# Weight splits on two engines instead of three, and layer-1 scores in fp32 row tiles

## Chip, core and metric

The kernel runs on one core of a Trainium2 chip. The metric is the device time of one launch in microseconds, from before the first instruction to after the last; the host's work on the layout of the weights is not in it. The kernel before takes 675.95 us (median of 3 runs, 675.43 to 677.0).

## The reference

The program is a decoder of two layers on one sequence of 256 tokens with 1024 features, in fp32. Layer 0 is stick-breaking attention with 16 heads of 64, layer 1 is native sparse attention (NSA) with 16 query heads over 4 key groups. Both have an MLP with a squared ReLU and 4096 hidden features. Keys and values of layer 1 come from the stream after layer 0. They feed three branches: 15 compressed blocks of 32 tokens (through a GELU MLP with `cmp_w1`), selected blocks, and a sliding window. With 256 tokens the top-16 choice takes all four blocks and the window of 512 takes all tokens, so the selected and the window branch are both plain causal softmax over their own keys.

```python
def stick_breaking_attention(h, w_qkv, w_o):
    ...
        z = jnp.einsum('bqhd,bshd->bhqs', q_blk, k).astype(jnp.float32) * scale
        causal = key_pos[None, :] < t[:, None]
        log_1m = jnp.where(causal, jax.nn.log_sigmoid(-z), 0.0)
        excl = lax.cumsum(log_1m, axis=3, reverse=True) - log_1m
        a = jnp.where(causal, jnp.exp(jax.nn.log_sigmoid(z) + excl), 0.0)
    ...
def nsa_attention(h, w_q, gate_b, w_o, shared):
    ...
        return jnp.stack([o_cmp, o_sel, o_win], axis=2).reshape(b, Q_BLOCK, 3, NSA_HEADS, DH)
    ...
    out = jnp.einsum('bsch,bschd->bshd', gates.astype(o.dtype), o).reshape(b, s, NSA_HEADS * DH)
    return out @ w_o
    ...
    for layer in range(DEPTH):
        hn = rms_norm(h, norm_gain[layer, 0])
        if layer < N_A_LAYERS:
            h = h + stick_breaking_attention(hn, sb_w_qkv[layer], sb_w_o[layer])
        else:
            j = layer - N_A_LAYERS
            h = h + nsa_attention(hn, nsa_w_q[j], nsa_gate_b[j], nsa_w_o[j], shared)
        h = h + sqrelu_mlp(rms_norm(h, norm_gain[layer, 1]), mlp_w1[layer], mlp_w2[layer])
        if layer == N_A_LAYERS - 1:
            shared = nsa_shared_kv(h, kv_norm, nsa_w_kv, cmp_pos, cmp_w1, cmp_w2)
```

## The kernel before

**Products and weights.** Large products are made of fp32r matmuls. A weight or an activation is split into a high part in fp32r and a low part, the rest; a product is then three matmuls, high by high, high by low and low by high (`mm3`, matmuls at L312). Weights are streamed by SP in tiles of 1 MB (128 x 2048 in fp32) into three buffers `raw`, in the order in which `feed` was called. Each tile is converted in two halves of 1024 columns: ACT casts the high part `wh` (L256), then DVE or POOL subtracts for the low part `wl` (L263). There are three pairs of wh and wl. The next transfer into a raw buffer is issued once the low part of the tile in it is done (`fetch`, called from `split`), and a tile's conversion waits until the tile three before it has been used by PE (`gone`).

**What sets the order.** PE's order is the order of the code. The order on DVE, ACT and POOL is worked out while the program is built: the class `Order` keeps a clock of its own, a queue of ready steps with ranks, and a cost in ns for each step on each engine that may take it, and it hands a step to the first engine that is free. `put` enters a step, `run` hands steps out, `tick` moves the clock by a matmul's cost and `need` waits for a chain of steps. The chosen order is then fixed in the program. The table `ways` says who may do a conversion: the low part goes to DVE or POOL, and to DVE alone inside the MLPs:

```python
        k = {"D": (150 + 1.045 * m, lo("D")), "G": (185 + 1.67 * m, lo("G"))}
        yield {e: k[e] for e in ways["lo"]}
```

**Stages.** Startup loads x and projects the values of layer 0. Layer 0 goes through the heads in groups of four: `proj` makes queries and keys of a head pair (48 fp32r matmuls `qk`, rotary step L617 into `qkT`), `scores` makes `z` in fp32, as two tiles of 64 rows side by side, `soft` is the stick-breaking softmax (ACT exp and log L633, DVE's evacuation L628, scan L634 and subtraction L635 on 128 x 774, ACT exp L637), `turn` transposes the result (`pa`, L324, copied to `sbt` at L674), and `values` makes `po` in two tiles of 64 columns, which L401 takes to `oT`.

An MLP runs over 8 blocks of 512 hidden features: `first(c)` makes two banks `pu` in 32 matmuls of 512 and 256 columns, `square` makes the squared ReLU and its high part hh (ACT L479) and low part hl (DVE L480), and `second(c)` adds 24 matmuls of 512 to the four banks `acc`. `second(c)` stands one block behind `first`: the code runs first(0), first(1), second(0), first(2), second(1), and so on, and the weights are fed in that order. Blocks 0 and 1 start with the half of the features of x that is transposed (`pt`) and normalised (`xn`, L383) first.

Layer 1 begins with three projections of 512 columns for the keys and values (`kv_proj`, `pk`); keys of the compressed branch are kept twice side by side. `gather_tr` and the following steps build the compressed blocks with their positions and split them into high and low parts; `cw_proj` multiplies them with cmp_w1 (`ph`, 64 matmuls, its weights split as all others), and `gelu` (`hx`, `hu` L1111) and `cmp_turn`, `cmp_kv` give the compressed keys and values. `q_proj` makes the queries of one key group in 48 matmuls (`qp`) and leaves them scaled (`qu`, L968), rotated (stream shuffle L974 and three steps on POOL, `qm`) and split in `qs` (L984). The heads go in eight pairs `p`, and the two heads of a pair share one key group. For a pair:

- `scores` makes `z` in 8 fp32r matmuls, with high and low parts stacked on the 128 rows;
- DVE adds the causal mask, writes `pe` and takes the maximum, in one instruction for each of 8 parts (L1020, `nm`);
- ACT takes 8 exps in SBUF (L1025), DVE inverts the sums (L1039) and multiplies them with the gates (L1041), and POOL (L1047) or DVE (L1048) scales `pe`;
- `turn` transposes `pe` in twelve blocks, four to a PSUM bank (`ptp`), in two steps of two banks and one bank, and ACT or DVE copies each bank to `pT` (L1073);
- `values` makes `po` from pT for two pairs, and `out_part` multiplies with the output weights (`acc`).

Between these steps stand other projections in the code, so that PE has work while a pair's softmax runs. Then come the second MLP and the final norm.

## Time and profile before

| what | value |
|---|---|
| median of 3 runs | 675.95 us (675.43 to 677.0) |
| the profiled execution | 676.55 us |
| its span, first to last instruction | 674.5 us |
| mean granted TensorE clock | 0.968 of full speed |
| PE busy | 625.9 us, 3506 matmuls |
| DVE busy | 450.4 us, 669 instructions |
| ACT busy | 343.4 us, 570 instructions |
| POOL busy | 166.7 us, 116 instructions |
| read from HBM | 106.60 MB, 160 GB/s over the span |

The span is shorter than the execution by 2.05 us, which lie ahead of the first and behind the last instruction. Names such as `wl` are the program's tiles, L263 is line 263 of the code, and `wl<-raw,wh` says that an instruction wrote wl from raw and wh. In a list of waits, `PE pa L324 <- ACT sbe L637: 5.1, 3, 3.1` says that PE, ahead of its transposes into pa, was idle for 5.1 us in 3 waits, 3.1 the longest, and that ACT's writing of sbe released it. In a chain, a row has the start, the length in us and the work. In a group, the number behind x is how many instructions there were, then come their busy time in us and the mean of one in ns; behind the second bar stand the idle time of the engine just before them and what ended it. In a table of stretches, the columns after the stretch are PE, its weight loads, DVE, ACT and POOL, each with busy us and the number of instructions, then the mean granted clock of TensorE, the busy share of the DMA engines and GB/s.

### The profile page before, as it was taken

To read this page: it belongs to the slowest core of one execution; us is meant where nothing else is said; L and a number is where in the kernel's file an instruction comes from. 1 tells how busy PE (TensorE), PEld (TensorE's weight loads), DVE (VectorE), ACT (ScalarE), POOL (GpSimd) and SP (SyncE) were. 2 spreads that over 40 slices of the span, in tenths; PEclk is the share of its full clock that TensorE was granted. 3 is DMA by queue.
4 is the path that set the end of the run, shared out by engine and by line. 5 is a ranking of instruction groups with operands and counts; after the bars stand their busy time and mean duration, and the time that the engine had idled before them with its cause. 6 is when DMAs were issued, how large, how long until landed. Compare 5 with 4: busy or idle time off the path is not lost.

```text
span 674.5 us, 8981 instructions
## 1 busy us (share of the span) xinstructions
PE 625.9 (93%) x3506; PEld 530.4 (79%) x3506; DVE 450.4 (67%) x669; ACT 343.4 (51%) x570; POOL 166.7 (25%) x116
## 2 busy tenths in 40 slices
PE   9998999989999999999996687699989999999995
PEld 6797978768888888888895676477768888888884
DVE  6378886556666656567898897675655666565654
ACT  4754564444554444446555655565444554445442
POOL 2654683100000000004689486324100000000000
PEclk9999999889999999999998878799989999999999
DMA  8963324335555555556445411102443545464501
GB/s 282 359 251 109 128 90 172 127 125 188 187 189 188 189 185 195 185 199 223 151 165 200 172 64 62 64 1 71 153 170 139 194 180 202 181 211 182 209 16 63
DMA packets 17322, 108.22 MB, mean 160 GB/s; under 512 B 2304, under 2 KB 3072, under 8 KB 4992
## 3 DMA queue, kind: packets, MB, share of 16 engines
q1 hardware_dynamic: 16848, 107.11, 44.4%
q8 instruction: 27, 0.44, 0.2%
q10 hardware_dynamic: 432, 0.55, 0.2%
q14 instruction: 15, 0.12, 0.1%
HBM read 106.60 MB, written 1.05 MB: 160 GB/s over the span
## 4 chain that ended last, share of the span: by engine, by line
PE 71%; DVE 14%; ACT 5%; POOL 5%; issue 3%; DMA 2%; SPq 0%; POOLq 0%; ACTq 0%; DVEq 0%
PE acc L312 31%; PE pu L312 26%; DVE wl L263 4%; ACT wh L256 2%; PE po L312 2%; PE qk L312 2%; PE qp L312 2%; PE pk L312 2%; DVE sbs L634 2%; DMA raw<-in_wv 2%; PE ptp L324 2%; PE pv L312 2%; DVE sbe L635 1%; PE z L312 1%; POOL wl L263 1%
## 5 line engine op out<-in xcount | busy, mean ns | idle before, releaser
L263 DVE TENSOR_TENSOR wl<-raw,wh 128x1024 fp32r<-128x1024 f32 (+1 forms) x159 | 208.0, 1324 | 130.1 <-ACT wh L256 127.6
L256 ACT CAST wh<-raw 128x1024 fp32r<-128x1024 f32 (+1 forms) x200 | 200.6, 1030 | 133.4 <-PE acc L312 62.4
L263 POOL TENSOR_TENSOR wl<-raw,wh 128x1024 fp32r<-128x1024 f32 (+1 forms) x41 | 107.1, 2623 | 249.2 <-ACT wh L256 246.6
L312 PE MATMUL pu<-xn,wh 128*128 128x512 f32 x512 | 131.5, 395 | 2.6 <-DVE xn L383 2.2
L312 PEld LDWEIGHTS pu<-xn,wh 128*128 128x128 f32 x512 | 93.9, 189 | 22.5 <-DVE xn L383 5.1
L312 PE MATMUL acc<-wh,hh 128*128 128x512 f32 x256 | 101.5, 396 | 5.1 <-ACT hh L479 5.1
L312 PE MATMUL acc<-wh,hl 128*128 128x512 f32 x256 | 101.2, 395 | 0.8 <-DVE hl L480 0.8
L312 PE MATMUL acc<-wl,hh 128*128 128x512 f32 x256 | 101.2, 395 | 0.0
L312 PEld LDWEIGHTS pu<-xn,wl 128*128 128x128 f32 x512 | 71.7, 192 | 5.8
L312 PE MATMUL pu<-xn,wl 128*128 128x256 f32 x512 | 73.4, 284 | 0.0
L312 PEld LDWEIGHTS acc<-wh,hh 128*128 128x128 f32 x256 | 49.0, 192 | 14.9 <-ACT hh L479 5.5
L312 PEld LDWEIGHTS acc<-wh,hl 128*128 128x128 f32 x256 | 48.8, 191 | 12.2 <-DVE hl L480 1.7
L312 PEld LDWEIGHTS acc<-wl,hh 128*128 128x128 f32 x256 | 48.9, 191 | 9.1
L479 ACT CAST hh<-ms 128x512 fp32r<-128x512 f32 x32 | 19.9, 621 | 62.6 <-DVE ms L478 62.6
L1346 POOL TENSOR_TENSOR r<-v,npow 128x1 f32<-128x1 f32 x2 | 1.5, 771 | 187.5 <-DVE v L1344 187.5
L312 PE MATMUL qk<-xa,wh 128*128 128x256 f32 x256 | 47.3, 286 | 0.0
L312 PE MATMUL acc<-wh,oT 128*128 128x512 f32 x128 | 43.8, 403 | 0.0
L312 PEld LDWEIGHTS qk<-xa,wh 128*128 128x128 f32 x256 | 39.7, 191 | 0.5 <-issue 0.3
L465 ACT COPY mr<-pu 128x256 f32<-128x256 f32 x64 | 23.6, 369 | 25.2 <-PE pu L312 25.2
L312 PE MATMUL qk<-xa,wl 128*128 128x256 f32 x128 | 36.2, 283 | 0.0
L480 DVE TENSOR_TENSOR hl<-ms,hh 128x512 fp32r<-128x512 f32 x32 | 22.1, 692 | 19.3 <-ACT hh L479 19.3
L466 DVE TENSOR_TENSOR mu<-pu,mr 128x256 f32<-128x256 f32 x64 | 26.6, 418 | 7.3 <-ACT mr L465 7.3
(178 smaller groups left out, 884.3 us busy)
## 6 DMA issues: line engine op xcount, KB each, us to landing
raw<-in_w SPq DMA_DIRECT2D x64, 1024.0 KB, 4.8
raw<-in_wqk SPq DMA_DIRECT2D x8, 1024.0 KB, 5.7
raw<-in_wo SPq DMA_DIRECT2D x8, 1024.0 KB, 4.9
raw<-in_wkv SPq DMA_DIRECT2D x6, 1024.0 KB, 4.8
raw<-in_wq SPq DMA_DIRECT2D x4, 1024.0 KB, 4.9
raw<-in_cw SPq DMA_DIRECT2D x4, 1024.0 KB, 4.7
raw<-in_wv SPq DMA_DIRECT2D x2, 1024.0 KB, 6.5
raw<-in_wv SPq DMA_DIRECT2D x3, 512.0 KB, 5.7
```

The costliest lines, as they stand in the source:

```text
L256: nc.scalar.copy(ws.made[j][0][:, r], ws.raws[j][:, r])
L263: (nc.vector if e == "D" else nc.gpsimd).tensor_sub(ws.made[j][1][:, r], ws.raws[j][:, r], f32(ws.made[j][0][:, r]))
L312: nc.tensor.matmul(o_, a, b, start=first, stop=last, skip_group_check=True)
L324: nc.tensor.transpose(o_, a, i)
L465: yield act(256, lambda: nc.scalar.copy(r[:, q], pu[f][:, 256:512]))
L466: yield dve(256, lambda: nc.vector.tensor_add(u[:, q], pu[f][:, 0:256], r[:, q]))
L479: yield act(512, lambda: nc.scalar.copy(hh, sv))
L480: yield dve(512, lambda: nc.vector.tensor_sub(hl, sv, f32(hh)))
L634: yield dve(774, lambda: nc.vector.tensor_tensor_scan(s[:, ::-1], s[:, ::-1], go_on[:, ::-1], 0.0, OP.add, OP.mult), 810)
L635: yield {"D": (956, lambda: nc.vector.tensor_sub(e, e, s)), "G": (1480, lambda: nc.gpsimd.tensor_sub(e, e, s))}
L1346: yield pool(1, lambda: nc.gpsimd.tensor_tensor(r, v, npow, op=OP.pow), 370)
```

## The change

The change has four parts.

1. **Low parts.** The low part of a weight is made on DVE only, in all stages, and so is the subtraction at the end of the stick-breaking softmax. The builder's queue also has two new rules: a step that reads and writes SBUF only on DVE (marked True) is not handed out while such a step of POOL runs, or the other way round (`port`), and steps of low rank can be held back for a time (`calm`).
2. **MLP.** `second` stands two blocks behind `first`: first(0), first(1), first(2), second(0), and so on, with two second products at the end; the weights are fed in that order.
3. **Layer 1, attention.** Queries and keys stay in fp32 and are not split. The two heads of a pair now come from two key groups (the host permutes the columns of the query and gate weights and the rows of the output weights to match), so that the two groups' keys lie one above the other in `kT`, and the scores of the two heads are fp32 matmuls in two tiles of 64 rows, in four PSUM banks. The causal mask is added by four bf16 matmuls (`z<-mask`). DVE takes the maxima from PSUM (L1064, four for a pair), ACT takes the exps from PSUM (L1058). Scaling is done apart for the two halves of the tokens (L1085 on POOL, L1086 on DVE), and `turn` transposes one bank at a time, in three steps, most of them into bank 2. Queries no longer take the scaling step (`qm`, L1016, is made from `qp` with a table that has the norm in it).
4. **Layer 1, projections.** The keys of the two causal branches are projected together, in 512 columns; their values in two projections of 256 columns (`v_proj`) that stand among the turns. The compressed weights are not split: `feed(..., True)` leaves the tile raw, no conversion is made, `cw_proj` takes it in fp32 matmuls of 256 columns in two tiles of 60 columns, and the next transfer into that raw buffer waits for PE. The compressed blocks are not split either.

```diff
+    def may(self, e, x):
+        if x[2][e][2] and self.port["G" if e == "D" else "D"] > self.t:
+            return False
+        return x[0] < 2 or self.calm[e] <= self.t
...
         wa, wb = [], []
         for c in range(NFC):
             wa.append(feed(w1[layer, c], 2048))
-            if c:
-                wb.append(feed(w2[layer, c - 1], 2048))
-        return wa, wb + [feed(w2[layer, NFC - 1], 2048)]
+            if c >= 2:
+                wb.append(feed(w2[layer, c - 2], 2048))
+        return wa, wb + [feed(w2[layer, c], 2048) for c in (NFC - 2, NFC - 1)]
...
+    feed_cw(0)
+    i_q.append(feed(wq[0], 2048))
+    feed_cw(1)
+    feed_cw(2)
+    i_q.append(feed(wq[1], 2048))
+    feed_cw(3)
+    i_vs.append(feed(wvs[0], 2048))
+    i_q.append(feed(wq[2], 2048))
+    i_vs.append(feed(wvs[1], 2048))
+    i_q.append(feed(wq[3], 2048))
...
-    ways = {"hi": "A", "lo": "DG"}
+    ways = {"hi": "A"}
...
-        k = {"D": (150 + 1.045 * m, lo("D")), "G": (185 + 1.67 * m, lo("G"))}
-        yield {e: k[e] for e in ways["lo"]}
+        yield {"D": (150 + 1.045 * m, lo, True)}
...
+        return ws.raws[i] if stream[i][2] else ws.made[i]
 
     def gone(i):
         assert ws.gone == i, (ws.gone, i)
         ws.gone += 1
+        if stream[i][2]:
+            fetch()
...
-        second(*held.pop(0), by_n)
         for c in range(2, NFC):
-            if c in (4, 6):
-                go(inverse_of(c // 2 - 2, r2), 3)
+            if c in (5, 7):
+                go(inverse_of((c - 5) // 2, r2), 3)
             st = begin(c)
             for f in range(2):
                 first(c, st, f, 0, NK)
             gone(wa[c])
             held.append((c, square(st)))
             second(*held.pop(0), by_n)
+        second(*held.pop(0), by_n)
...
-            yield dve(774, lambda: nc.vector.tensor_tensor_scan(s[:, ::-1], s[:, ::-1], go_on[:, ::-1], 0.0, OP.add, OP.mult), 810)
-            yield {"D": (956, lambda: nc.vector.tensor_sub(e, e, s)),
-                   "G": (1480, lambda: nc.gpsimd.tensor_sub(e, e, s))}
+            yield dve(774, lambda: nc.vector.tensor_tensor_scan(s[:, ::-1], s[:, ::-1], go_on[:, ::-1], 0.0, OP.add, OP.mult), 810, True)
+            yield {"D": (956, lambda: nc.vector.tensor_sub(e, e, s), True)}
...
-        def cw_proj(c, i):
+        def cw_proj(n):
+            c, i = divmod(n, 2)
+            o.need(gc_[c])
+            w = W(i_c[c][i])
+            o.tick(90)
             for jj in range(8):
-                w = W(i_c[c][i], jj // 4)
                 j = 8 * i + jj
-                q = ph[:, c * 256:(c + 1) * 256]
-                wh, wl = cut(w, jj * 256, (jj + 1) * 256)
-                mm(q, blk[c][:, j].rearrange("p a m -> p (a m)"), wh, c == 0 and j == 0, False)
-                mm(q[0:DH, :], blk[c][:, j, 0, :], wl, False, j == 15)
+                r = slice(jj % 2 * DH, jj % 2 * DH + M)
+                mm(ph[r, c * 256:(c + 1) * 256], blk[c][:, j, :], w[:, jj * 256:(jj + 1) * 256],
+                   c == 0 and j < 2, j >= 14, 2.0)
+            o.tick(90)
             gone(i_c[c][i])
...
             for hd in range(2):
-                for i in range(2):
-                    mm(z1[hd], x[:, j, hd, P:2 * P], kT[i][:, g, :, :], i == 0, i == 1)
+                r = slice(hd * DH, (hd + 1) * DH)
+                mm(z1[hd], x[r, j, P:2 * P], kT[r, p // 4, :, :], True, False, 2.0)
             for hd in range(2):
-                for i in range(2):
-                    mm(z0[:, hd], x[:, j, hd, 0:P], kT[i][:, g, :, 0:P], hd == 0 and i == 0, i == 1)
...
+            low = mask[:, P:2 * P][:, None, :].to_broadcast([P, 2, P])
+            for z in (z1[0][:, :, P:2 * P], z1[1][:, :, P:2 * P], *z0):
+                mm(z, mask[:, 0:P], low, False, True)
...
+            def ex(hd, t, b):
+                if t:
+                    d, z, i = pe[:, hd, b * 256:(b + 1) * 256], z1[hd][:, b, :], 4 + 2 * hd + b
+                else:
+                    d, z, i = pe[:, hd, 512 + b * P:512 + (b + 1) * P], z0[hd][:, b, :], 2 * hd + b
+                n = P * (t + 1)
+                return act(n, lambda: nc.scalar.activation(
+                    d, z, AF.Exp, bias=nm[:, i:i + 1], accum_out=rs[:, t, hd, b:b + 1]), 150)
+
+            def unit(hd, t):
+                i = 4 * t + 2 * hd
+                z = (z0, z1)[t][hd]
+                yield dve(256 * (t + 1), lambda: nc.vector.tensor_reduce(nm[:, i:i + 2], z, axis=AX.X, op=OP.max, negate=True))
+                yield [ex(hd, t, b) for b in range(2)]
+
+            uc = [go(unit(hd, t), 1 + 0.01 * p) for t in (1, 0) for hd in range(2)]
...
-                def low(t, b):
-                    d, z, m, n = part(t, b)
-                    return dve(n, lambda: nc.vector.tensor_tensor_reduce(
-                        d, z, m, 1.0, -NEG, OP.add, OP.min, nm[:, 2 * t + b:2 * t + b + 1]), 60)
-
-                def ex(t, b):
-                    d, z, m, n = part(t, b)
-                    return act(n, lambda: nc.scalar.activation(
-                        d, d, AF.Exp, bias=nm[:, 2 * t + b:2 * t + b + 1], scale=-1.0, accum_out=rs[:, hd, t, b:b + 1]), 150)
...
-        def turn(p, banks, part):
+        def turn(p, i, bank):
...
-            for i in (2,) if part else (0, 1):
-+            if True:
+                pt = B(bank, "ptp")
```

The instructions of the engines now stand in another order. On DVE, in layer 0, from the evacuation of the scores of group 1 to the splits ahead of group 2's, before:

```order
L628 TENSOR_TENSOR sbe<-z,cst 128x3x128 x4
L634 SCALAR_TENSOR_TENSOR sbs<-sbs,go_on 128x774
L401 TENSOR_TENSOR oT<-po,oT 128x512
L634 SCALAR_TENSOR_TENSOR sbs<-sbs,go_on 128x774
L617 TENSOR_TENSOR qkT<-qk,rbq 128x512
L635 TENSOR_TENSOR sbe<-sbe,sbs 128x774
L617 TENSOR_TENSOR qkT<-qk,rbq 128x512
L674 COPY sbt<-pa 128x512 x2
L263 TENSOR_TENSOR wl<-raw,wh 128x1024
```

At the same place after the change (the line numbers are those of the changed code: L660 was L628, L666 was L634, L667 was L635, L298 was L263):

```order
L660 TENSOR_TENSOR sbe<-z,cst 128x3x128 x4
L666 SCALAR_TENSOR_TENSOR sbs<-sbs,go_on 128x774
L435 TENSOR_TENSOR oT<-po,oT 128x512
L667 TENSOR_TENSOR sbe<-sbe,sbs 128x774
L649 TENSOR_TENSOR qkT<-qk,rbq 128x512
L666 SCALAR_TENSOR_TENSOR sbs<-sbs,go_on 128x774
L298 TENSOR_TENSOR wl<-raw,wh 128x1024
L667 TENSOR_TENSOR sbe<-sbe,sbs 128x774
L298 TENSOR_TENSOR wl<-raw,wh 128x1024
L649 TENSOR_TENSOR qkT<-qk,rbq 128x512
L705 COPY sbt<-pa 128x512
L298 TENSOR_TENSOR wl<-raw,wh 128x1024 x2
```

Both subtractions `sbe` of the group and four splits `wl` now stand in DVE's row; before, one subtraction and the greater part of the splits were in POOL's.

On PE, at the first second product of the first MLP, before (`pu` are the banks of first, `acc` those of second; the numbers tell single tiles apart):

```order
L312 MATMUL pu_1237<-xn,wh 128x512 x4
L312 MATMUL pu_1237<-xn,wl 128x256 x4
L312 MATMUL acc_1326<-wh,hh 128x512
L312 MATMUL acc_1326<-wl,hh 128x512
L312 MATMUL acc_1326<-wh,hl 128x512
```

And after:

```order
L346 MATMUL pu_1237<-xn,wh 128x512 x4
L346 MATMUL pu_1237<-xn,wl 128x256 x4
L346 MATMUL pu_1312<-xn,wh 128x512 x8
L346 MATMUL pu_1312<-xn,wl 128x256 x8
L346 MATMUL pu_1313<-xn,wh 128x512 x8
L346 MATMUL pu_1313<-xn,wl 128x256 x8
L346 MATMUL acc_1373<-wh,hh 128x512
L346 MATMUL acc_1373<-wl,hh 128x512
L346 MATMUL acc_1373<-wh,hl 128x512
```

The 32 matmuls of block 2's first product now stand between block 1's and the first second product.

On DVE, in layer 1, around the softmax of pairs 0 and 1, before:

```order
L968 TENSOR_TENSOR qu<-qp,rbn 128x512
L1111 TENSOR_TENSOR hu<-hu,hx 60x512
L974 STREAM_SHUFFLE qw<-qu 128x512
L1039 RECIPROCAL rs<-rs 128x8
L1041 TENSOR_TENSOR rs<-rs,gates 128x8
L1048 TENSOR_TENSOR pe<-pe,rs 128x512 x2
L1039 RECIPROCAL rs<-rs 128x8
L1073 COPY pT<-ptp 128x512 x2
L1041 TENSOR_TENSOR rs<-rs,gates 128x8
L1048 TENSOR_TENSOR pe<-pe,rs 128x512
L984 TENSOR_TENSOR qs<-qm,qs 64x2x256 x2
```

And after, from the scaling sums of pair 0 to the maxima of pair 1:

```order
L298 TENSOR_TENSOR wl<-raw,wh 128x1024
L1073 RECIPROCAL rs<-rs 128x4 x2
L298 TENSOR_TENSOR wl<-raw,wh 128x1024
L1016 TENSOR_TENSOR qm<-qp,rbc 128x512
L1075 TENSOR_TENSOR rs<-rs,gates 128x4 x2
L1018 STREAM_SHUFFLE qw<-qu 128x512
L1064 TENSOR_REDUCE nm<-z_3098 128x2
L1064 TENSOR_REDUCE nm<-z_3099 128x2
L1064 TENSOR_REDUCE nm<-z_3100 128x2
L1064 TENSOR_REDUCE nm<-z_3101 128x2
L1086 TENSOR_TENSOR pe<-pe,rs 128x2x256
```

The masks L1020 and the split L984 are gone from DVE's row, the four maxima of a pair and the splits `wl` of the streamed weights stand in it.

More of the change, by code (lines that the diff above doesn't have):

```diff
@@ L80, in run @@
                         moved = True
-            ts = [self.free[e] for e in self.free if any(e in x[2] for x in self.ready)]
+            ts = [y for e in self.free if any(e in x[2] for x in self.ready)
+                  for y in (self.free[e], self.calm[e], *self.port.values())]
             ts += [x[0] for x in self.events[:1]]
@@ L222, in fetch @@
             return
-        src, n = stream[j]
+        src, n, whole = stream[j]
         raw = wp.tile([P, n], F32, tag="raw", name="raw", bufs=3)
@@ L242, in split @@
             yield ws.his[2 * j + half - 1]
-        while ws.gone < j - NB + 1:
+        before = [i for i in range(j) if not stream[i][2]]
+        while len(before) >= NB and ws.gone <= before[-NB]:
             w = Waiter()
@@ new lines, in layer1, with among @@
+        cw_proj(0)
+        kT = ap.tile([P, 2, 2, T * P], F32, name="kT")
+        q_proj(0, 7)
+        gc_[1] = gather_tr(1, 5)
+        cw_proj(1)
+        for t in range(T):
+            kc.append(keys_tr(t, 2 + t))
+        gT = gate_proj(1)
+        def among(f, cuts, p, banks):
+            for i, (k0, k1) in enumerate(zip((0, *cuts), (*cuts, NK))):
+                f(k0, k1)
+                if i < len(banks):
+                    turn(p, i, banks[i])
+        scores(0, Z)
+        cw_proj(2)
@@ L1259, in layer1 @@
+        part(0, 0)
         cmp["s1"] = cmp_soft(1, *cmp["s1"], 7)
[L1260 to L1271 removed]
```

491 lines of the change are left out of this document (252 added, 239 removed).

## Prediction

> **What bounds the kernel now.** I read the waits of PE first, since PE is busy 93% of the span, then the chain that ended last, then the groups of instructions on DVE and POOL in single stages.
>
> ```profile
> PE 625.9 (93%) x3506; PEld 530.4 (79%) x3506; DVE 450.4 (67%) x669; ACT 343.4 (51%) x570; POOL 166.7 (25%) x116
> ...
> PE pa L324 <- ACT sbe L637: 5.1, 3, 3.1
> ...
> PE ptp L324 <- DVE pe L1048: 7.3, 2, 3.7
> PE ptg L324 <- DVE gT L916: 6.5, 1, 6.5
> PE ptp L324 <- POOL pe L1047: 5.7, 4, 4.4
> ...
> PE acc L312 <- ACT hh L479: 2.5, 1, 2.5
> ```
>
> The first row is the page's, the next is from PE's waits up to 126 us (layer-0 attention), the rest from 310 to 510 us (layer-1 attention and the start of the second MLP). So PE bounds everything except three kinds of place: the stick-breaking softmax, the layer-1 softmax, and the first second product of each MLP. Inside an MLP nothing is left to take: PE goes from block to block without a gap, as the chain shows (its last two rows; behind them a group of the page).
>
> ```profile
> 30.09 14.39 PE qk L312 x120
> ...
> 44.48 0.90 PE z L312 x8
> ...
> 93.80 1.51 PE z L312 x16
> ...
> 98.25 1.45 PE po L312 x16
> ...
> 125.62 3.92 PE pu L312 x13
> 129.54 0.87 PE pt L324 x8
> ...
> 142.47 6.88 PE acc L312 x22
> 149.35 5.56 PE pu L312 x32
> 154.91 5.47 PE acc L312 x24
> ...
> L256 ACT CAST wh<-raw 128x1024 fp32r<-128x1024 f32 (+1 forms) x200 | 200.6, 1030 | 133.4 <-PE acc L312 62.4
> ```
>
> These rows also price PE. An fp32r matmul of 512 columns takes 5.47/24 = 0.228 us, one of 256 columns 14.39/120 = 0.120, a transpose 0.87/8 = 0.109. The fp32 scores of layer 0 (`z`, two 64-row tiles side by side) take 1.51 us for 1536 output columns; the fp32 `po` (two 64-column tiles side by side) takes 1.45 for 1536, or 0.94 ns a column.
>
> **MLP starts: the second product two blocks behind.** From 125.62 to 149.35 are 23.73 us. The work there is 64 first-product matmuls (2 x 5.56 = 11.12), 8 transposes (0.87) and one second product (5.47), 17.46 in all, so 6.27 us are lost: about 3 as a wait for hh and hl of block 0, the rest as slow clock. The stretches below (busy us of PE, PEld, DVE, ACT, POOL, then the granted clock) show that slow clock arrive after little idleness.
>
> ```profile
> 124.00:125.00 1.00, 0.50 (x1) 0.19 (x1) 1.00 (x2) 1.00 (x2) 0.00 (x0) 1.00 0.63 221
> 125.00:126.00 1.00, 0.38 (x2) 0.30 (x2) 1.00 (x3) 0.73 (x1) 0.00 (x0) 0.95 1.02 434
> 126.00:127.00 1.00, 1.00 (x6) 1.00 (x5) 1.00 (x2) 0.00 (x0) 0.00 (x0) 0.50 0.81 336
> ...
> 485.24 2.37 PE pu L312 x13
> ...
> 507.50 5.56 PE pu L312 x32
> ```
>
> The second MLP has the same place from 485.24 to 507.50: 22.26 us for the same 17.46, so 4.8 lost. With block 2's first product (5.56 us) put ahead, hh and hl of block 0 have more than the 3 us that they lacked. What is late next is w1 of block 2: it now converts in the place in the stream that w2 of block 0 had, and that one was ready before the wait began; w2 of block 0 follows one product later. At the end two second products stand back to back; each needs one weight tile per 5.47 us, and a tile costs ACT 2 x 1.03 (the page's group of `wh`) and DVE 2 x 1.22 us (the group of `wl` from 150 to 300 us, below). I take 5.4 + 4.4 = **9.8 us**, leaving 0.9 and 0.4 because the wait for the last xn ahead of both starts stays and may still lower the clock once. The bounds are 7 (only the idle goes) and 11.1.
>
> The Trainium skill, "TensorE: Matmul & The Clock Gate", section "Why this matters for your kernels", says to allow no PE idle gaps over about 3 us, one idle window being what halves the clock. The trace differs: PE was idle a little over 1 us in the stretch 124 to 126 and then ran at 0.50.
>
> **No weight splits on POOL, layer 0.** Groups of DVE and POOL from 28 to 126 us, then the same DVE line from 150 to 300 us, where POOL does nothing, and two single pieces of the chain at times when POOL was idle:
>
> ```profile
> L263 DVE TENSOR_TENSOR wl<-raw,wh 128x1024 fp32r<-128x1024 f32 x11 | 21.5, 1963 | 6.4 <-ACT wh L256 3.9 <-POOL wl L263 2.5
> L634 DVE TENSOR_TENSOR_SCAN sbs<-sbs,go_on 128x774 f32<-128x774 f32 x8 | 21.1, 2639 | 4.9 <-ACT sbs L633 4.9
> L635 DVE TENSOR_TENSOR sbe<-sbe,sbs 128x774 f32<-128x774 f32 x4 | 8.9, 2213 | 0.1
> ...
> L263 POOL TENSOR_TENSOR wl<-raw,wh 128x1024 fp32r<-128x1024 f32 x17 | 47.6, 2815 | 24.9 <-ACT wh L256 24.3 <-PE pr L312 0.6
> ...
> L263 DVE TENSOR_TENSOR wl<-raw,wh 128x1024 fp32r<-128x1024 f32 x56 | 67.4, 1222 | 54.5 <-ACT wh L256 54.5
> ...
> 48.26 1.77 DVE sbs L634
> ...
> 57.37 0.98 DVE sbe L635
> ```
>
> A POOL tile of 2.8 us therefore costs DVE 0.74 us on each of its splits, 0.87 on a scan and 1.23 on a subtraction that it lies beside. The change gives DVE 17 more splits (20.8 us) and 4 subtractions (3.9), and takes that slowing away. What counts is the path from one `z` to the next. Between the first rows of group 0's and group 3's scores lie 93.80 - 44.48 = 49.3 us; PE's own work there is 5.5 projections of 48 x 0.120, 36 transposes, two `po` and three `z`: 31.7 + 3.9 + 2.9 + 4.5 = 43.0. DVE's new order from the first `z` evacuation of a group to that of the next, after 2.9 us until the first scan (in the chain the first `z` ends at 44.48 + 0.90 and the scan begins at 48.26), has two scans, two subtractions, four splits, two qkT and up to two copies and one oT (0.69 each, as the copy `pT` below): 14.6, 16.0 and 14.2 us for the three groups, 44.8 in sum. DVE thus becomes about as long as PE. I take 49.3 to 45.8, **3.5 us**; bounds: a gain of 6.3 (PE's sum) and a loss of 15.5 (the same order at the slowed durations: 6 scans, 6 subtractions and 10 splits add 20). Behind the late splits waits PE's projection of the next pair, which has its tile a whole projection ahead. Startup's two POOL halves move into gaps of DVE; I count nothing there, since the weight DMAs set that stage, with 0.8 either way.
>
> **Layer 1.** The stage from the first `pk` to the last wait for xn:
>
> ```profile
> 310.08 2.73 PE pk L312 x12
> ...
> 452.07 1.40 PE z L312 x8
> ...
> 454.85 3.62 PE po L312 x40
> ...
> 360.00:440.00 80.00, 54.93 (x353) 47.97 (x352) 65.40 (x164) 44.26 (x120) 47.96 (x29) 0.81 0.30 105
> ```
>
> It lasts 485.24 - 310.08 = 175.2 us. PE's work before: 144 `pk` 32.8, 192 `qp` 23.0, 144 transposes 15.7, 64 `ph` 7.7, 8 scores of 1.40 11.2, 4 values of 3.62 14.5, 96 `acc` 21.9, 8 `gp` 1.8, small ones about 3.7: 132.3. So **42.9 us are lost**, 25.1 as idle of PE between 360 and 440 us alone (the last row) and most of the rest at that stretch's clock of 0.81.
>
> PE's work after: the values' projection in 96 matmuls of 256 instead of 48 of 512, +0.6; 16 transposes fewer, -1.7; `ph` as 32 fp32 matmuls of 256 columns in two column tiles at 0.94 ns a column, 7.7, the same; scores 1.51 (the same 1536 columns as layer 0's `z`) plus 4 mask matmuls of 0.12, 1.99 against 1.40, +4.7. Sum **+3.6**. Bounds: the mask matmuls could be free (-3.8) or, like the row tiles, not overlap (a rival below).
>
> What goes is the long way to each transpose. Nearest rows for the new steps (DVE's and ACT's groups, 300 to 510 us):
>
> ```profile
> L1025 ACT ACTIVATE pe<-pe,nm 128x256 f32<-128x256 f32 x32 | 15.9, 500 | 0.0
> ...
> L1025 ACT ACTIVATE pe<-pe,nm 128x128 f32<-128x128 f32 x32 | 12.5, 391 | 0.0
> L1020 DVE CUSTOM_DVE_ANT_0 pe<-z,cst 128x256 f32<-128x256 f32 x32 | 12.2, 414 | 0.8 <-PE z L312 0.7
> ...
> L1047 POOL TENSOR_TENSOR pe<-pe,rs 128x512 f32<-128x512 f32 x7 | 8.7, 1241 | 4.6 <-ACT pe L1025 4.5
> ...
> L1073 DVE COPY pT<-ptp 128x512 f32<-128x512 f32 x10 | 6.9, 688 | 4.2 <-PE ptp L324 4.2
> ...
> L1041 DVE TENSOR_TENSOR rs<-rs,gates 128x8 f32<-128x8 f32 x8 | 3.6, 456 | 0.2
> ...
> L1039 DVE RECIPROCAL rs<-rs 128x8 f32<-128x8 f32 x8 | 1.6, 196 | 6.2 <-ACT pe L1025 6.2
> ```
>
> A pair needs a maximum over 512 (as a PSUM read of 512, 0.69), eight exps (4 x 0.50 + 4 x 0.39 = 3.6), reciprocal and gate (0.20 + 0.46) and a scale on POOL (1.24): about 6.2 us. PE's new order puts 9.5 us (pair 7: two parts of 1.37, three transposes of four, 24 `acc`) to 13.8 us (pair 0: two `ph` of 1.93, 48 `qp`, scores, 18 `pk`) between a pair's scores and its first transposes. The chain is covered by 3 to 7 us. The splits of qs and of the blocks and the masks on DVE are gone, and POOL's splits with them.
>
> What is late next, with what remains (R): each pair has three groups of four transposes, and 9 of the 24 groups follow upon one in the same PSUM bank with only 12 matmuls (1.44 us) or less between; the copy (0.69) that they wait for stands behind up to one split (1.22) or two exps (1.0), and I take 0.7 each, 6. The scales of pairs 0 and 3 stand on DVE behind two splits: 2. The exp of the gates stands on ACT behind pair 0's eight exps and DVE waits for it, 1.5. POOL keeps 16 scales and 8 query steps, about 30 us; where a quarter lies beside a split, DVE gives 2.5. One more lowered clock, 1.7. **R = 14** (13.7, rounded); bounds 4 (copies always in time, and no more than two of the other items) and 30 (1 us at each of the 24 groups, and the 5.7 behind them). So layer 1 gains 42.9 - 3.6 - 14 = **25.3 us**. The compressed weights leave ACT 8 casts and DVE 8 splits lighter, which these waits already assume; their raw buffers are now freed by PE, but the next DMAs have over 8 us before use.
>
> Sum: 9.8 + 3.5 + 25.3 = 38.6. The profiled execution took 676.55 (span 674.5 and 2.05 around it), 0.6 above the median of 675.95: 676.55 - 38.6 = 637.95, on the median's scale 637.4, forecast **637**.
>
> **Rivals.** (1) The copies are in time and nothing cools, R = 4: 627. For: DVE's load falls by more than what the splits add. (2) Short gaps do not lower the clock, as the skill's gate rule would have it: 0.9, 0.4 and 1.7 us go, 634; against it stands the 0.50 row. (3) Copies and maxima queue behind splits in DVE's fixed order, R = 30: 653. (4) The change does not do what it says: row and column tiles do not run side by side; 8 x 1.5 and 7.7 us more, 657. Layer 0's `z` and `po` speak against it. (5) Slower: the single bank. If each of the 24 transpose groups waited 2.5 us with the clock it costs, R = 60: 683. It turns slower at R = 52.6, 2.2 us a group; ACT's and DVE's queues hold that much only if three items are always ahead.
>
> **How the numbers follow.** Chances: forecast 0.52 (its own range 629 to 646), (1) 0.14, (2) 0.08, (3) 0.19, (4) 0.04, (5) 0.03. The range 626 to 655 leaves out (4), (5) and some of (1) and (3). About 0.2% is what a measurement of this kernel can tell from no change: faster 0.96, same 0.01, slower 0.03.
>
> **What would show it.** In the MLPs, 32 `pu` between block 1 and the first `acc`, and no PE wait for hh. In layer 0, splits on DVE of 1.22 us, scans of 1.77, subtractions of 0.98, POOL idle. In layer 1, scores near 2.0 us, `ph` near 1.9 for eight, PE waits of `ptp` under 1 us each and fewer stretches at 0.50. Scores of 3 us, DVE splits still above 1.6 us, or PE waiting 2 us at each `ptp`, would make the prediction wrong.

## The result and the profile after

The changed kernel takes 628.2 us (median of 4 runs, 626.71 to 629.31), the kernel before 675.69 on the same chips (4 runs). The ratio is 0.929, with a 95% interval of 0.927 to 0.932: 47.5 us faster. The forecast was 637, the range 626 to 655. The profiled execution took 626.71 (span 624.9).

The first row is the page's on busy time (us, share of the span, instructions), the second its row of TensorE's granted clock in 40 slices, in tenths of full speed.

```profile
PE 611.7 (98%) x3570; PEld 514.2 (82%) x3570; DVE 424.4 (68%) x606; ACT 328.9 (53%) x556; POOL 43.6 (7%) x58
...
PEclk9999999999999999999999999999999999999998
```

PE is busy for 98% of the span, and every slice but the last has 9. What is left of PE's waits, from 0 to 118 us, 118 to 298, 297 to 441 and 441 to 625 (us in total, times, the longest):

```profile
PE warm L346 <- DVE zero L371: 1.2, 1, 1.2
PE pa L358 <- ACT sbe L668: 0.9, 1, 0.9
...
PE pu L346 <- DVE xn L417: 0.9, 1, 0.9
PE pt L358 <- DVE hres L443: 0.7, 1, 0.7
...
PE pu L346 <- DVE xn L417: 1.1, 2, 0.6
PE ptp L358 <- ACT pT L1111: 0.9, 1, 0.9
PE po L346 <- DVE pT L1111: 0.3, 1, 0.3
...
PE pu L346 <- DVE xn L417: 0.6, 1, 0.6
```

The waits for hh and for the exponentials' scaling are gone, and the 24 groups of transposes `ptp` make PE wait once. Now the rows of the chain that stand at the stages' borders (start, length, work), as those that the prediction quotes for the kernel before:

```profile
43.50 1.51 PE z L346 x16
...
88.15 1.51 PE z L346 x16
...
118.86 2.37 PE pu L346 x13
...
122.10 14.01 PE pu L346 x80
136.11 5.47 PE acc L346 x24
...
297.63 2.72 PE pk L346 x12
...
412.40 2.04 PE z L346 x12
...
440.74 2.74 PE pu L346 x14
```

From these borders the time can be split into stages. The table does it for all kernels, with the same rows of each one's chain: the first scores of layer 0, the scores of group 3, the first `pu` of the first MLP, the first `pk`, the first `pu` of the second MLP, the end of the span. The name of an experiment begins with b where it changes the kernel before, with a where it changes the changed kernel. All in us; the median is of that kernel's runs.

| kernel | startup | layer 0, z to z | to MLP 1 | MLP 1 | layer 1 | MLP 2, end | span | median |
|---|---|---|---|---|---|---|---|---|
| before | 44.5 | 49.3 | 31.8 | 184.5 | 175.2 | 189.3 | 674.5 | 675.7 |
| after | 43.5 | 44.7 | 30.7 | 178.8 | 143.1 | 184.2 | 624.9 | 628.2 |
| b_mlp2 | 44.4 | 49.3 | 31.8 | 179.4 | 177.0 | 183.9 | 665.8 | 667.5 |
| b_nopool | 44.1 | 44.7 | 30.7 | 183.8 | 168.4 | 188.9 | 660.5 | 661.2 |
| b_both | 44.8 | 44.7 | 30.7 | 178.8 | 167.4 | 183.9 | 650.2 | 652.0 |
| b_warm | 45.9 | 50.1 | 31.8 | 182.9 | 176.8 | 187.5 | 675.0 | 674.5 |
| a_one | 43.8 | 44.7 | 30.7 | 183.8 | 143.1 | 189.2 | 635.3 | 637.2 |
| a_pool | 43.9 | 52.3 | 31.3 | 179.8 | 153.6 | 184.2 | 645.1 | 647.8 |
| a_vearly | 47.6 | 44.7 | 30.7 | 178.8 | 159.2 | 185.7 | 646.7 | 644.1 |
| a_cwsplit | 45.2 | 44.7 | 30.7 | 178.8 | 150.4 | 184.2 | 634.0 | 634.5 |
| a_turn3 | 43.7 | 44.7 | 30.7 | 178.8 | 156.1 | 184.1 | 638.0 | 641.1 |
| a_noport | 44.5 | 44.7 | 30.7 | 178.8 | 143.2 | 184.2 | 626.1 | 627.9 |
| a_nomask | 43.3 | 44.7 | 30.7 | 178.8 | 141.0 | 184.2 | 622.6 | 625.4 |

A reader should see how steady the columns are: where a stage's code is the same, it repeats within 0.2 us in nearly all rows. The startup spreads, from 43.3 to 47.6, with 0 to 3.6 us of waits for the first weights. Four more entries differ by 0.8 to 1.8 us without an edit in their stage: layer 0 and layer 1 of b_warm, layer 1 of b_mlp2, and the last stage of a_vearly. A difference of stages therefore says more than one of totals. Between before and after the stages give 1.0, 4.7, 1.1, 5.7, 32.1 and 5.1 us, in sum 49.6.

One stretch of layer 1 and the whole stage (PE, weight loads, DVE, ACT, POOL, each busy us and instructions; granted clock, DMA share, GB/s):

```profile
352.00:380.00 28.00, 28.00 (x223) 23.88 (x222) 27.75 (x52) 18.74 (x52) 13.80 (x10) 1.00 0.34 121
...
297.63:440.74 143.11, 140.60 (x985) 111.29 (x984) 111.07 (x206) 82.43 (x216) 38.13 (x37) 1.00 0.38 138
```

In 28 us DVE is busy for 27.75, and PE has no gap in them. The whole stage has 2.5 us without PE, at a mean clock of 1.00; before, 27.3 of 175.2 us were without PE.

### The profile page after: what moved, and what is told of

Read it like the earlier page. It is cut to its first block, busy times and chain, and to the rows that moved or that the text cites. A ratio compares the mean times of both kernels' runs of the same rounds, so it can differ in the third digit from the quotient of the medians.

```text
span 624.9 us, 8905 instructions
## 1 busy us (share of the span) xinstructions
PE 611.7 (98%) x3570; PEld 514.2 (82%) x3570; DVE 424.4 (68%) x606; ACT 328.9 (53%) x556; POOL 43.6 (7%) x58
## 4 chain that ended last, share of the span: by engine, by line
PE 82%; DVE 10%; DMA 2%; ACT 2%; issue 2%; SPq 0%; POOL 0%; POOLq 0%; ACTq 0%; DVEq 0%
PE acc L346 32%; PE pu L346 28%; PE qk L346 7%; DVE wl L298 4%; PE pk L346 3%; PE po L346 3%; PE z L346 2%; PE pv L346 2%; ACT wh L292 1%; DVE nm L1064 1%; DMA raw<-in_wq 1%; PE qp L346 1%; PE ph L346 1%; DMA raw<-in_wv 1%; PE pa L358 1%
## 5 line engine op out<-in xcount | busy, mean ns | idle before, releaser
L298 DVE TENSOR_TENSOR wl<-raw,wh 128x1024 fp32r<-128x1024 f32 (+1 forms) x192 | 227.6, 1206 | 109.8 <-ACT wh L292 107.4
L292 ACT CAST wh<-raw 128x1024 fp32r<-128x1024 f32 (+1 forms) x192 | 193.3, 1031 | 127.8 <-PE acc L346 54.3
L346 PE MATMUL pu<-xn,wh 128*128 128x512 f32 x512 | 130.1, 392 | 2.0 <-DVE xn L417 1.9
L346 PE MATMUL acc<-wh,hh 128*128 128x512 f32 x256 | 100.0, 391 | 0.0
L346 PE MATMUL acc<-wl,hh 128*128 128x512 f32 x256 | 99.9, 390 | 0.0
L346 PE MATMUL acc<-wh,hl 128*128 128x512 f32 x256 | 99.6, 389 | 0.0
L346 PE MATMUL pk<-wh,xk 128*128 128x512 f32 (+1 forms) x128 | 33.6, 342 | 0.0
L1058 ACT ACTIVATE pe<-z,nm 128x256 f32<-128x256 f32 (+1 forms) x64 | 26.1, 429 | 11.6 <-DVE nm L1064 11.4
```

What stands on the lines that cost most here:

```text
L292: nc.scalar.copy(ws.made[j][0][:, r], ws.raws[j][:, r])
L298: nc.vector.tensor_sub(ws.made[j][1][:, r], ws.raws[j][:, r], f32(ws.made[j][0][:, r]))
L346: nc.tensor.matmul(o_, a, b, start=first, stop=last, skip_group_check=True)
L1058: return act(n, lambda: nc.scalar.activation(d, z, AF.Exp, bias=nm[:, i:i + 1], accum_out=rs[:, t, hd, b:b + 1]), 150)
```

## The experiments

**Parts of the change one by one: b_mlp2, b_nopool, b_both.** In b_mlp2 the kernel before gets the new order of the MLP:

```diff
-            if c:
-                wb.append(feed(w2[layer, c - 1], 2048))
-        return wa, wb + [feed(w2[layer, NFC - 1], 2048)]
+            if c >= 2:
+                wb.append(feed(w2[layer, c - 2], 2048))
+        return wa, wb + [feed(w2[layer, c], 2048) for c in (NFC - 2, NFC - 1)]
...
-        second(*held.pop(0), by_n)
         for c in range(2, NFC):
...
+        second(*held.pop(0), by_n)
```

> The kernel before with one part of the change: the second product of each MLP stands two blocks behind the first. Theory (the wait for hh and hl and the slow clock that follows it both go): between the first pu of an MLP and block 2's work 6.3 and 4.8 us were lost, so 675.7 - 11 = 664.7 us, and no stretch at a clock of 0.50 near the start of either MLP. Rival (only the idle time goes, the slow clock has another cause): 675.7 - 5.4 = 670.3 us, with the clock still at 0.50 somewhere in the first 25 us of an MLP.

It came to 667.5 us (ratio 0.987, 0.985 to 0.990). The two MLPs gained 5.1 and 5.4 us, nearly what the theory asked for, and nothing waits for hh any more; layer 1 lost 1.8. Of that, 1.3 are a longer wait of PE for `ce` of the compressed branch (2.7 us against 1.4). b_warm has the same 2.7; no edit touches that place, and why the wait grew stays open. One thing was not as expected: the wait for xn ahead of the first MLP stayed, and slow clock behind it. PE's wait and two stretches of b_mlp2:

```profile
PE pu L312 <- DVE xn L383: 1.1, 1, 1.1
```

```profile
125.00:126.00 1.00, 0.48 (x3) 0.44 (x4) 1.00 (x3) 0.63 (x1) 0.00 (x0) 1.00 1.04 442
126.00:128.00 2.00, 2.00 (x9) 1.71 (x8) 1.73 (x2) 0.00 (x0) 0.00 (x0) 0.53 0.29 123
```

In b_nopool the kernel before makes all low parts and the softmax's subtraction on DVE:

```diff
-    ways = {"hi": "A", "lo": "DG"}
+    ways = {"hi": "A", "lo": "D"}
...
-            yield {"D": (956, lambda: nc.vector.tensor_sub(e, e, s)),
-                   "G": (1480, lambda: nc.gpsimd.tensor_sub(e, e, s))}
+            yield {"D": (956, lambda: nc.vector.tensor_sub(e, e, s))}
```

> The kernel before with one part of the change: low parts of weights and the softmax's subtraction on DVE only; nothing else. Theory (what POOL's splits cost is the slowing of DVE, and it is paid where DVE sets the pace, in layer 0): layer 0 gains 3.5 to 5 us, splits of 1.2 us, scans of 1.76 and subtractions of 0.96 there; layer 1 keeps most of its waits, since they come from the length of the softmax chain, and gains 0 to 8: 663 to 672 us. Rival (POOL's splits caused most of layer 1's waits too): layer 1 falls from 175 to 155 us or less, 645 to 655 us in all. Second rival (DVE becomes the bound of layer 1, with 41 more splits of which 15 or so stand there): slower than 676.

It took 661.2 us (ratio 0.978, 0.974 to 0.981), 14.5 less than before's 675.7: layer 0 gained 4.7 and 1.1 up to the MLP, layer 1 gained 6.8, near the upper end of the theory, and PE's long waits there stayed. The first rival (most of layer 1) and the second (slower) fell.

b_both has both edits.

> The kernel before with two parts of the change: low parts and the softmax's subtraction on DVE only, and the second product two blocks behind. What is then left to the changed kernel is the new layer 1. Theory (the two parts work in different stages and add up): 675.9 - 15.6 - 9.3 = 651 us, 649 to 653, with layer 1 at 168 to 170 us; the new layer 1 is then worth 21 to 25 us. Rival (they overlap): above 654.

It took 652.0 us (ratio 0.965, 0.963 to 0.967): the parts add up. Layer 1 stands at 167.4, so the new layer 1 is worth the 24.3 us between it and the changed kernel's 143.1. What it still waits for, from 297 to 467 us:

```profile
PE ptp L324 <- DVE pe L1047: 11.5, 4, 6.6
PE ptg L324 <- DVE gT L915: 4.1, 1, 4.1
PE pct L324 <- DVE ce L1186: 3.1, 1, 3.1
...
```

**The same parts undone: a_one, a_pool.** a_one takes b_mlp2's edit back out of the changed kernel.

> The changed kernel with one part undone: the second product stands one block behind the first again. Theory (idle and slow clock come back together): 628.2 + 11 = 639 us, with a wait of PE for hh of 2.5 to 3 us and a stretch at 0.50 after it in both MLPs. Rival (only the idle comes back): 628.2 + 5.4 = 633.6. Second rival (without POOL's work the hh chain is shorter, and less than 3 us come back): 630 to 631.

It took 637.2 us (ratio to before 0.943, 0.939 to 0.947), 9 above the changed kernel, and both MLPs lost 5.0 us. PE's waits in its first MLP, and two stretches of it:

```profile
PE acc L346 <- ACT hh L513: 2.4, 1, 2.4
...
PE acc L346 <- DVE hl L514: 0.5, 1, 0.5
```

```profile
125.00:137.00 12.00, 9.10 (x43) 7.27 (x42) 8.46 (x12) 6.31 (x10) 0.00 (x0) 0.89 0.29 107
137.00:138.00 1.00, 1.00 (x4) 0.76 (x4) 0.00 (x0) 0.00 (x0) 0.00 (x0) 0.56 0.71 98
```

2.9 us are the two waits; the other 2.1 of the 5.0 come behind them, with a clock of 0.56 in the stretch shown. The second rival (a shorter chain without POOL) fell.

a_pool lets POOL make low parts again, outside the MLPs, and the softmax's subtraction:

```diff
+PT = True
...
-        yield {"D": (150 + 1.045 * m, lo, True)}
+        k = {"D": (150 + 1.045 * m, lo("D"), PT), "G": (185 + 1.67 * m, lo("G"), PT)}
+        yield {e: k[e] for e in ways["lo"]}
```

> The changed kernel with one part undone: low parts of weights outside the MLPs, and the softmax's subtraction, may go to POOL again, whichever is free first in the builder's queue. Theory (each POOL split slows the DVE work beside it): DVE's splits go from 1.2 to 1.6 us and more, layer 0 loses 4.6 us and layer 1 5 to 15, since its DVE is full in 352 to 380 us and its transposes then wait for scales and copies: 638 to 648 us. Rival (POOL relieves a full DVE and the sum is the same): 628 to 633 us.

It took 647.8 us (ratio to before 0.959, 0.956 to 0.961), 19.6 above the changed kernel: layer 0 lost 7.6, more than the theory's 4.6, and layer 1 10.4. In layer 0 the loss arrives at PE through the softmax: ahead of its transposes `pa` PE waits 6.8 us, against 0.9 in the changed kernel.

```profile
PE pa L365 <- ACT sbe L678: 6.8, 2, 5.0
```

The groups of DVE in a_pool from 43.9 to 96.2 us, and the same two lines of the changed kernel from 27 to 118 (busy us, mean ns):

```profile
L675 DVE TENSOR_TENSOR_SCAN sbs<-sbs,go_on 128x774 f32<-128x774 f32 x6 | 14.3, 2392 | 3.9 <-ACT sbs L674 3.9
L676 DVE TENSOR_TENSOR sbe<-sbe,sbs 128x774 f32<-128x774 f32 x4 | 11.1, 2784 | 0.2
```

```profile
L298 DVE TENSOR_TENSOR wl<-raw,wh 128x1024 fp32r<-128x1024 f32 x26 | 30.8, 1217 | 4.3 <-ACT wh L292 4.3
L666 DVE TENSOR_TENSOR_SCAN sbs<-sbs,go_on 128x774 f32<-128x774 f32 x8 | 14.0, 1763 | 2.9 <-ACT sbs L665 2.9
...
L667 DVE TENSOR_TENSOR sbe<-sbe,sbs 128x774 f32<-128x774 f32 x8 | 7.6, 956 | 0.0
```

In that stretch of a_pool DVE makes no split at all, and still its own steps are late: a subtraction takes 2784 ns where it takes 956 alone. The difference, 1.83 us, is less than one POOL split (2.88 us on average from 27 to 128 us). The Trainium skill, "SBUF — State Buffer", section "SBUF: two separate sides", says that a DVE step with two inputs from SBUF and a GpSimd step that reads SBUF shut each other out, the later one waiting for the other's whole length; the lengths here agree with that. DVE's copies out of PSUM keep their length in the same stretch (`sbt`, 686 ns in a_pool, 682 in the changed kernel). So POOL's help bought DVE nothing: in a_pool it has 572 instructions and is busy for 422.8 us, in the changed kernel it has 606 and is busy for 424.4. One reservation: the rule `port` stands in a_pool too and shifts the builder's order there, so its 19.6 us may hold something of that; the 14.5 us of b_nopool are free of it.

**What carries the new layer 1: a_vearly, a_turn3, a_cwsplit.** The three take one thing each out of the new layer 1. a_vearly projects the values ahead of the pairs, takes these projections out from among the turns of pairs 0 and 2, and feeds their weights in the new order:

```diff
+        v_proj(0, 1, 0, NK)
+        v_proj(1, 6, 0, NK)
         rbc = spread(4)
...
-        among(lambda k0, k1: v_proj(0, 1, k0, k1), (3, 5, 7), 0, (2, 2, 2))
+        for i in range(3):
+            turn(0, i, 2)
```

> The changed kernel, but the two projections of the values (48 matmuls of 256 columns each for either branch's two token tiles, 23 us of PE in all with their weights' splits) stand ahead of the softmax pairs, behind the keys' projection, as they did before, and the turns of pairs 0 and 2 follow without them. Theory (DVE is busy 99% from 352 to 393 us and PE hides it only because these projections stand there): PE now runs out of other work there, and layer 1 grows by 8 to 15 us: 636 to 643, with waits of PE for DVE (pT, pe, hu). Rival (the shorter softmax chain alone carries layer 1): 628 to 631, with PE still without waits.

It took 644.1 us (ratio to before 0.952, 0.948 to 0.957), and layer 1 grew by 16.1 us, a little more than the theory had. PE's longest waits there, and the middle of layer 1:

```profile
PE qp L345 <- DVE vcb L1187: 3.6, 1, 3.6
PE ptp L357 <- DVE pT L1110: 2.6, 4, 0.8
...
```

```profile
349.00:410.00 61.00, 49.92 (x343) 38.31 (x343) 45.85 (x95) 34.77 (x108) 23.59 (x18) 0.92 0.37 136
```

DVE is busy for only 75% of this stretch, and yet PE is idle for 11.1 of its 61 us: the work that PE had beside DVE's is now at another place. In the whole stage, 10.1 of the 16.1 us are more idle time of PE, 6.0 its slower work. The work moved is smaller than the expectation has it: 96 matmuls of 0.120, 11.5 us and not 23.

a_turn3 leaves the projections where they are and puts the three turns of pairs 0 to 4 one behind the other, in one bank:

```diff
-        turn(1, 0, 2)
         q_proj(2, 7, 3, 5)
-        turn(1, 1, 2)
         cmp["tc"] = cmp_turn(0)
         q_proj(2, 7, 5, NK)
+        turn(1, 0, 2)
+        turn(1, 1, 2)
         turn(1, 2, 2)
```

> The changed kernel, but the three groups of transposes of pairs 0 to 4 stand one behind the other, where the last of them stood, all in one PSUM bank, and no other matmuls lie between them. Theory (a group must wait for the copy of the one before: 0.69 us of copy, some 0.3 of hand-over, and what stands ahead on DVE or ACT): 10 waits of 1 to 2 us, and slow clock behind some of them: 12 to 24 us slower, 640 to 652. Rival (PE's queue of other work absorbs them): under 4 us.

It took 641.1 us (ratio to before 0.949, 0.945 to 0.953), layer 1 grew by 12.9: 8.2 us more idle time of PE and 4.7 more busy time. There are ten waits of the kind that the theory named, 0.9 us each where it had 1 to 2:

```profile
PE ptp L358 <- DVE pT L1111: 6.9, 7, 1.4
PE ptp L358 <- ACT pT L1111: 2.1, 3, 0.7
```

a_cwsplit converts the compressed weights again, without use of the result (two more lines of the edit let a conversion count these tiles among those it waits for, and let the next transfer be issued behind the conversion):

```diff
-            ws.parts.append(Chain(o, whole_part(j, h) if whole else split(j, h), rank_of(j), ws.landed))
+            ws.parts.append(Chain(o, split(j, h), rank_of(j), ws.landed))
```

> The changed kernel, but the compressed weights are converted again as all others (8 casts of 1.03 us on ACT, 8 subtractions of 1.22 on DVE), while cw_proj still takes the raw tile: the results of the conversion are not used. Theory (DVE has no room from 345 to 393 us, but 12 us from 298 to 337): half of the conversions meet the full stretch, and 2 to 6 us come back: 630 to 634. Rival (all hidden): within 1 us of 628.2. Second rival (each microsecond of DVE shows): 9.8 us, 638.

It took 634.5 us (ratio to before 0.937, 0.933 to 0.940), and layer 1 grew by 7.3. The sum lies at the theory's upper edge, but not for its reason. The timeline ahead of pair 0's scores (start, length, work; in brackets the idle time before):

```profile
333.19 0.33 SPq L260 DMA_DIRECT2D raw<-in_cw  x1
...
338.04 1.04 ACT L292 CAST wh<-raw 128x1024 fp32r<-128x1024 f32 x1 [4.91 <-DMA raw<-in_cw]
338.99 0.58 ACT L923 COPY kT<-ptk 128x512 f32<-128x512 f32 x1
...
339.67 3.02 PE L344 MATMUL z<-kT,qm 64*128 64x512 f32 x8 [3.63 <-issue]
```

The cast of the next compressed tile stands on ACT ahead of the copy of the keys, and its tile is still on the way: ACT waits 4.9 us for the transfer, the copy behind it is late, and the scores start 0.1 us after the copy's end and take 3.02 us for what takes 1.56 in the changed kernel's timeline. This one wait is 3.6 of the 4.9 us by which PE's idle time in the stage grew. The transfer itself is no later than in the changed kernel: it is issued 33.8 us after the stage's first `pk` in both. DVE had room at that place (33.1 us busy of the 40.6 from 299.4 to 340). So in this order the unsplit weights take a wait for a transfer out of ACT's row, which none of the three theories had. An order in which the copy stands first was not tried, so what the conversions cost by themselves stays open.

**Two small prices: a_noport, a_nomask.** a_noport takes the rule `port` out of the builder; a_nomask leaves the mask matmuls out, so that every token sees all keys.

```diff
-        if x[2][e][2] and self.port["G" if e == "D" else "D"] > self.t:
-            return False
```

> The changed kernel with the builder's rule for steps of DVE and POOL on SBUF (port) taken out; the order of DVE and POOL then comes from ranks and costs alone. Theory (what counts is that POOL has no splits; 16 scales and 8 query steps are all that the rule can move): within 1.5 us of 628.2. Rival (the rule, not the missing splits, keeps PE supplied in layer 1): 632 to 640.

It took 627.9 us (ratio 0.930, 0.927 to 0.932): the rule is worth nothing that can be measured here.

```diff
-            for z in (z1[0][:, :, P:2 * P], z1[1][:, :, P:2 * P], *z0):
-                mm(z, mask[:, 0:P], low, False, True)
```

> The changed kernel without the four mask matmuls of each pair: the causal mask of layer 1 is left out. It prices them: theory (PE is the bound of layer 1 again, and 4 x 0.12 lie open): 8 x 0.5 = 4 us faster, 623.5 to 625. Rival (DVE's full stretch from 352 to 393 us sets the pace, and the matmuls stand in its shade): 627 to 628.5.

It took 625.4 us (ratio 0.927, 0.924 to 0.930). The intervals of the two ratios overlap, so the total can't tell it from the changed kernel. By the stage of the profiled executions it is 2.1 us, between theory and rival: PE's busy time in layer 1 falls by 3.2 (140.60 to 137.38 us) and its idle time rises by 1.1.

**What slows the clock: b_warm.** In the kernel before, PE gets 12 matmuls of no use in the place where it waits for hh:

```diff
+        keep = B(accs[0], "keep")
+        for i in range(12):
+            mm(keep, x_[0][:, 0, 0:P], x_[2][:, 0, :, :], True, True)
         second(*held.pop(0), by_n)
```

> The kernel before, with 12 more fp32r matmuls of 512 columns (12 x 0.228 = 2.7 us) in each MLP ahead of the first second product, in the place where PE waits for hh; they write a bank that the second product then starts afresh, so nothing else changes and the wait itself stays as long. Theory (a wait of under 3 us lowers PE's clock for the matmuls behind it): in each MLP the lost 5.05 us are 2.9 of idle and 2.1 of slow clock; with PE busy through the wait the 2 x 2.1 go, 4 us faster than before, 671.7 to 673 us, and no stretch at 0.5 to 0.6 behind the wait. Rival (the slow clock does not come from the wait): no change, 675.5 to 676.8, with the slow stretch still there. Second rival (the added matmuls cost their own time): 2 x 2.7 us slower, 681.

The median is 674.5 against 675.9 us (ratio 0.998, 0.995 to 1.000), short of the theory's gain (671.7 to 673). In the profiled execution the startup, layer 0 and layer 1 were 1.4, 0.8 and 1.7 us longer than in that of before, where nothing was edited. The MLPs' stages are 1.6 and 1.7 us shorter, 3.3 of the 4 expected. The stretches behind the wait, of before and then of b_warm:

```profile
143.00:144.00 1.00, 1.00 (x4) 0.72 (x3) 1.00 (x2) 0.62 (x1) 0.00 (x0) 0.50 0.59 238
144.00:145.00 1.00, 1.00 (x4) 0.81 (x3) 0.75 (x2) 0.00 (x0) 0.00 (x0) 0.50 0.00 0
145.00:146.00 1.00, 1.00 (x3) 0.78 (x3) 0.00 (x0) 0.00 (x0) 0.00 (x0) 0.50 0.96 131
```

```profile
144.00:145.00 1.00, 0.99 (x4) 0.51 (x5) 1.00 (x2) 0.00 (x0) 0.00 (x0) 1.00 0.98 418
145.00:146.00 1.00, 1.00 (x6) 0.83 (x5) 1.00 (x2) 0.62 (x1) 0.00 (x0) 1.00 0.68 279
```

Three or four matmuls in a us became four to six. The second product starts 16.1 us after the first `pu`, 0.4 later than before, and runs at full speed. So it is the wait that lowers the clock here, and filling it, even with work of no use, takes away most of the second part of its price.

## Why the prediction was right, and where its sizes were off

The forecast was 637 and the time 628.2: inside the range, 0.8 below the forecast's own lower end of 629. Of the cases on record it is the first rival (copies in time, nothing cools, 627; given 0.14) that came, not the forecast's own waits. In the stages of the profiled executions 49.6 us were gained, against a sum of 38.6.

**MLP starts: 9.8 on record, 10.1 measured** (2 x 5.0 between after and a_one; 5.1 and 5.4 in b_mlp2). The step was right, and its wait was sized right: about 3 us on record, 2.9 measured, with 2.1 of slow clock behind it in each MLP. The 6.27 and 4.8 us that it reads as lost are some 0.7 too small, since three of the 64 `pu` matmuls stand ahead of the rows it starts from (three of 0.228 us at 123.00 in the first MLP); the gain was not taken from that. What was off is the reason for the 0.9 and 0.4 held back: the wait for xn stays (0.9 us), but no slow clock follows it now. That part is luck as far as these runs show: at this place waits of the same length were followed by slow clock in some cases and not in others (the last section has them).

**Layer 0: 3.5 on record, 4.7 measured**, 44.65 us from z to z where the sum of PE's work was 43.0 and that of DVE 44.8 (which comes out with ten splits in the three groups, as in the bound beside it, not with four in each); on the three scans, splits and subtractions the durations on record (1.77, 1.22, 0.98) came out as 1.76, 1.22 and 0.96. The part behind it, up to the MLP, gained 1.1, and the first MLP 0.6 besides the new order; both were counted at nothing. b_nopool has the same 44.7, 30.7 and 0.6, so the low parts off POOL give all of it without the other parts of the change. Behind the 0.6 stand 1.4 us of slow clock that did not come (the 13 `pu` behind the wait for xn take 2.37 us, in b_mlp2 3.74) and a new wait of 0.7 for hres.

**Startup: nothing on record, 1.0 measured.** Its spread over the kernels (43.3 to 47.6 us) is larger than that, so it is no effect of the change that these runs show.

**Layer 1: 25.3 on record, 32.1 measured.** This is the term that was mis-sized, in R, the waits that remain: 14 us on record, 7.2 by the same sum. The trace shows only 2.5 us of idle PE and no slow clock; the other 4.7 are work, 140.6 us of busy PE at a clock of 1.00 where the count gave 135.9. Which item the count had too small was not looked into. PE's work for the scores was sized right (2.04 us a pair, 1.99 on record), so was `ph` (1.87, 1.93).

The items of R came out so: the copies 0.9 us in one wait, not 6, and 0.3 ahead of one `po`; the scales of pairs 0 and 3 none, not 2; the gates none, not 1.5; POOL beside the splits none, not 2.5 (DVE's 29 splits in the stage took 1.27 us on average); one more lowered clock none, not 1.7. Another 1.1 of the 2.5 us is the wait for xn. The step that failed is the 0.7 us at each of nine groups: "the copy (0.69) that they wait for stands behind up to one split (1.22) or two exps (1.0)". Three of the 24 copies do begin 1.6 to 1.9 us after the end of their transposes, the others within 1.0, but only one of the three stands where PE needs the bank soon. It stands behind four exps of ACT (pair 3 in the timelines of PE and ACT):

```profile
381.69 0.60 PE L358 MATMUL ptp<-ident,pe 128*128 128x128 f32 x4
...
384.22 0.59 ACT L1111 COPY pT<-ptp 128x512 f32<-128x512 f32 x1
...
384.86 0.66 PE L358 MATMUL ptp<-ident,pe 128*128 128x128 f32 x4 [0.92 <-ACT pT L1111]
```

On the chain of a pair the prediction was too short. Pair 1 in the timeline of the changed kernel, its scores, its scales on POOL and its first transposes:

```profile
345.78 0.61 PE L346 MATMUL z<-mask 128*128 128x256 bf16 x4
...
352.50 3.58 POOL L1085 TENSOR_TENSOR pe<-pe,rs 128x512 f32<-128x512 f32 x3 [1.90 <-DVE rs L1075]
...
359.72 0.60 PE L358 MATMUL ptp<-ident,pe 128*128 128x128 f32 x4
```

The scores end at 346.4 us and the last scale at 356.1, 9.7 us later (on record 6.2); the transposes start at 359.7, 13.3 us after the scores. Read in the same way, the chain is 13.2 us in pair 0, 9.6 to 10.7 in pairs 1 to 3, 5.8 to 8.7 behind them. The cover was sized right: 9.4 us (pair 7) to 14.6 (pair 4), on record 9.5 to 13.8. So it held in every pair, with 1.0 us to spare in pair 0 and 3.1 to 5.9 in the others, where the record has 3 to 7. In b_both, pair 1's scores end at 363.4 and its last scale at 382.5, 19.1 us later, and PE waits 6.6 us for it; the chain did get shorter. What the work among the turns is worth a_vearly and a_turn3 show: without it layer 1 is at 159 and 156 us.

**The rivals.** Short gaps that don't cool (the second) fell as a rule, though its 634 is nearer to the time than the forecast is. The Trainium skill, "TensorE: Matmul & The Clock Gate", section "Why this matters for your kernels", allows idle gaps up to about 3 us. The trace differs: a_one's 2.4 and 0.5 us halved the clock, and by b_warm it is such waits that do it. Tiles that do not run side by side (the fourth) fell with 2.04 and 1.87 us. The single bank (the fifth) is a real mechanism, at 0.9 us a wait in a_turn3, but the matmuls that the change puts between two groups keep it from PE but for one wait of 0.9. R = 30 (the third) fell with 2.5 us of idle PE.

**What the parts are worth.** In the kernel before: the MLP's order 10.4 us in its two stages, low parts off POOL 14 us in all stages (13.6 without the startup), the new layer 1 the rest, 24 (b_both to after). Undone from the other side, POOL costs 19.6 and the MLP's order 9. Within layer 1 the pieces do not add: projections among the turns 16.1, turns apart 12.9, unsplit compressed weights 7.3, no POOL 10.4 are 47 in sum, against 32 for the stage. A likely reason, not shown, is that each keeps PE supplied for the others; and the price of the compressed weights holds the one wait of ACT's order. How much of the 24 is the shorter softmax chain (no masks on DVE, no splits of the queries) was not tried by itself.

## What to carry to other kernels

Price a helper engine by what it does to the engine beside it: POOL took splits off DVE and made DVE's steps on two inputs in SBUF up to three times as long in that time, on the path that set the pace. Price a wait of PE with the slow clock behind it, here a fifth (a_pool's layer 1: 8.6 us more idle, 1.9 more busy) to three quarters (a_one: 2.9 and 2.1) of its length again, and look for work to put into it before looking for a shorter wait. Where one engine's row is full, PE need not wait for it as long as other matmuls stand at that place: moving 11.5 us of them away cost 16.
